# Moving the first attention block's query path into the DFT stage, with the latents' loads and one sequence's output-weight gating

## The chip, the cores and the metric

One core of a Trainium2 chip. The core has a matrix engine (PE, with its weight loads shown as PEld), a vector engine (DVE), an activation engine (ACT), a general engine (POOL) and a sync engine (SP) that here only issues transfers. Each engine takes its instructions in the order of its own queue and waits on semaphores. The metric is the device time of one execution in microseconds.

## The reference

Two sequences of 1024 tokens and width 1024 go through one layer. A conditioning vector gives shift, scale and gate for each half of the layer. Attention (4 heads, low-rank queries and keys, a rotary part) and a 2-D Fourier mixing run side by side on the same normed input:

```
mod = jax.nn.silu(c) @ w_ada + b_ada            # sh1, sc1, ga1, sh2, sc2, ga2
h = rmsnorm(x, g_mix) * (1.0 + sc1) + sh1
z = h @ w_in                                    # q_lat 256, kv_lat 128, k_pe 64, f_in 512
y_mla = mla_group(q_lat, kv_lat, k_pe, ...)     # softmax attention, 4 heads
y_four = fourier_group(f_in, w_four)            # Re(fft2) over tokens and 64 channels, then w_four
x = x + ga1 * (concat(y_mla, y_four) @ w_out)
x = x + ga2 * ((silu(h2 @ w_gate) * (h2 @ w_up)) @ w_down)   # h2: normed and modulated x
```

A last rmsnorm gives the outputs. All is 32-bit floating point.

## The kernel before

Each product is made of three matmuls on values split into a high and a low part: mm3 (lines 70 to 73), and split (59 to 61), in which ACT casts the high part and DVE subtracts to get the low one. The kernel runs in stages that keep their results in DRAM buffers.

Stage 1 (both sequences, 8 pairs of row blocks) norms, transposes and projects. It writes the latents to lat_d (128 partitions, two 128-row pieces of query latents, one of key latents, one of the rotary key), the values to ckv_d, the folded query weights to wq_d, the folded output weights without gate to wo_d, and the gate rows to ga_d.

Stage 2 is the DFT stage (pools p2a on the left of the on-chip memory, p2 and praw on the right). For each sequence s it runs dft(s), prep_wm(s), which loads and splits Fourier output weights through eight "raw" buffers, and fourier_out(s, abn, j) for j = 1, 2, 3, 0 (lines 690 to 719). One fourier_out has two groups g of 13 matmuls into two of eight PSUM banks. ACT copies one bank (ea, L706), DVE forms difference and sum (ed, three buffers each), and SP stores both to fo_d (L719). Beside the first sequence's four steps run the chunks of the second modulation vector (wada2, four buffers of 1 MB in p2a, lines 742 to 749). After dft(1) and prep_wm(1) the left pool is closed, and pool p3e takes its bytes. stage3_loads (lines 581 to 596) then loads the first block's query latents (ql), the query weights wq in two halves through two "hv" buffers with a split each, the rotary tables rc and rs, and, by load_seq(0), the first sequence's latents (2 x 1 MB) and values (2 x 512 KB).

Stage 3 is attention. The items are (sequence, block of 256 rows, head, half): 64 of them. Item k runs scores; one item later its probabilities are transposed (flip_p), then multiplied with the values; out_proj follows 11 items behind. Before the loop, rope_q (L842 to 860) forms the rotary part of the queries of block (0, 0), absorb_q the folded query of head 0, and rope_flip transposes the rotary part. In the loop the same functions run ahead for later blocks. The table todo gives other work to items: at items 0 and 2, gate_half(0, g) loads a gate row of 128 copies into one buffer (gah), and wv_load(0, g) loads four pieces of wo_d and multiplies each with it on POOL (L958, L959); wv_split splits the eight results into wv at items 3 to 10. add_x starts accumulating transfers from POOL.

The order on each queue is not that of the text. A scheduler orders the instructions by priority when the program is built, gives a tile the first buffer of its tag that comes free, and sets the waits. A tile whose buffer is held by another waits for the last user of that one. issue_after(i) places what is under it behind instruction i on its engine. Each transfer also waits until the eighth transfer before it on its queue is done, since eight semaphores go round.

Of the kernel before, what the change touches and what calls it, by code (L numbers as in the profile page):

```python
# [12 lines left out]
F32 = mybir.dt.float32  # L13
# [37 lines left out]
def hybrid_encoder_kernel(ctx: ExitStack, tc: tile.TileContext, a: dict):  # L51
# [513 lines left out]
    def load_seq(s, lp=None):  # L565
        lat = [(e if s == 0 else lp).tile([P, 2, N], F32R, tag=f"lat{s}{i}", name=f"lat{s}{i}") for i in range(2)]
        ckv = [e.tile([P, 8, KVL], F32R, tag=f"ckv{i}", name=f"ckv{i}", bufs=1) for i in range(2)]
        for i in range(2):
            nc.sync.dma_start(rd(lat[i]), lat_d[s][i][:, 2:4, :])
        for i in range(2):  # L570
            nc.sync.dma_start(rd(ckv[i]), ckv_d[s][i])
        S[s] = (lat, ckv)

    def load_q(s, b):
        ql = [e.tile([P, 2, 256], F32R, tag=f"ql{i}", name=f"ql{i}", bufs=2) for i in range(2)]
        for i in range(2):
            nc.sync.dma_start(rd(ql[i]), lat_d[s][i][:, 0:2, 256 * b : 256 * b + 256])
        S["q", s, b] = ql

    def stage3_loads():  # L580
        wq_h = e.tile([P, 2, 768], F32R, name="wq_h")
        wq_l = e.tile([P, 2, 768], F32R, name="wq_l")
        load_q(0, 0)
        for c in range(2):
            wqr = half("wqr")
            wqr2 = half("wqr2")
            nc.sync.dma_start(wqr, wq_d[:, c, 0:512])
            nc.sync.dma_start(wqr2[:, :256], wq_d[:, c, 512:768])
            split(wq_h[:, c, 512:768], wq_l[:, c, 512:768], wqr2[:, :256])
            split(wq_h[:, c, 0:512], wq_l[:, c, 0:512], wqr)  # L590
        rc = e.tile([P, 8, ROPE], F32, name="rc")
        nc.sync.dma_start(rc, a["ropec"])
        rs = e.tile([P, 8, ROPE], F32, name="rs")
        nc.sync.dma_start(rs, a["ropes"])
        load_seq(0)
        return wq_h, wq_l, rc, rs

    with ExitStack() as st:
# [4 lines left out]

        def bank2():
            return pp.tile([P, 512], F32, tag="b", name="bank")

        zh, wms = {}, {}

# [82 lines left out]
        def fourier_out(s, ABn, j):  # L691
# [5 lines left out]
            for g in range(2):  # L697
# [20 lines left out]
                for u in range(2):  # L718
                    nc.sync.dma_start(fo_d[s][rows(j, u), gs], ed[u])  # L719

        zsplit(0)
        tb[1] = [wa.tile([P, 4, 512], F32R, name=f"tb1{i}") for i in range(2)]
        for c in range(4):
# [113 lines left out]
    with ExitStack() as st:  # L837
# [4 lines left out]
        def rope_q(s, b, u):  # L842
            ql = S["q", s, b]
            ti = 2 * b + u
            us = slice(u * P, u * P + P)
            pq = gbank()
            for c in range(2):
                mm3(pq[:, :256], ql[0][:, c, us], ql[1][:, c, us], wq_h[:, c, 512:], wq_l[:, c, 512:], c == 0, c == 1)
            pv = pq[:, :256].rearrange("p (h r) -> p h r", h=HEADS)
            t1 = half("qt1").rearrange("p (k h r) -> p k h r", k=2, h=HEADS)  # L850
            cb = rc[:, ti : ti + 1, :].broadcast_to([P, HEADS, ROPE])
            sb = rs[:, ti : ti + 1, :].broadcast_to([P, HEADS, ROPE])
            nc.vector.tensor_tensor(out=t1[:, 0], in0=pv, in1=cb, op=ALU.mult)
            nc.vector.tensor_tensor(out=t1[:, 1, :, :32], in0=pv[:, :, 32:], in1=sb[:, :, :32], op=ALU.mult)
            nc.vector.tensor_tensor(out=t1[:, 1, :, 32:], in0=pv[:, :, :32], in1=sb[:, :, 32:], op=ALU.mult)
            here["p"] = nc.gpsimd.tensor_tensor(out=t1[:, 0], in0=t1[:, 0], in1=t1[:, 1], op=ALU.add).ins
            sk = w.tile([P, HEADS, P], F32R, tag="sk", name="qsk", bufs=2)
            nc.scalar.copy(sk[:, :, :64], t1[:, 0])
            nc.vector.tensor_tensor(out=sk[:, :, 64:], in0=t1[:, 0], in1=rd(sk[:, :, :64]), op=ALU.subtract)
            S["sk", s, b, u] = sk  # L860

        def rope_flip(s, b, u):
            sk = S.pop(("sk", s, b, u))
            pt = tbank("pqt", F32R)
            for h in range(HEADS):
                nc.tensor.transpose(pt[:, h, :], sk[:, h, :], identr)
            qp = w.tile([P, HEADS, P], F32R, tag="qp", name="qp", bufs=4)
            nc.scalar.copy(qp, rd(pt))
            S["qp", s, b, u] = qp

        def absorb_q(s, b, h):
            ql = S["q", s, b]
            pq = gbank()
            hs = slice(h * P, h * P + P)
            for c in range(2):
                mm3(pq[:, :256], wq_h[:, c, hs], wq_l[:, c, hs], ql[0][:, c, :], ql[1][:, c, :], c == 0, c == 1)
            qa = [w.tile([P, 256], F32R, tag=f"qa{i}", name=f"qa{i}", bufs=3) for i in range(2)]
            split(qa[0], qa[1], pq[:, :256])
            S["qa", s, b, h] = qa

        def scores(s, b, h, u):
            lat = S[s][0]
            qa, qp = S["qa", s, b, h], S["qp", s, b, u]
# [69 lines left out]
        def wv_load(s, g):  # L953
            gs = slice(512 * g, 512 * g + 512)
            raw4 = (w if s == 0 else e).tile([P, 4, 512], F32, tag=f"lat{1 - s}{g}", name="wvr4")
            for h in range(HEADS):
                raw = raw4[:, h, :]
                nc.sync.dma_start(raw, wo_d[:, h, gs])  # L958
                nc.gpsimd.tensor_tensor(out=raw, in0=raw, in1=S["ga"], op=ALU.mult)  # L959
                S["wv", h, g] = raw  # L960

        def wv_split(i):
# [20 lines left out]
        for k in range(nit + 4):  # L983
            if k >= nit:
                i = k - nit
                out_proj(1, 2, i // 2, i % 2)
                if i == 1:
                    norm2(1, 2, 0, tl)
            if k < nit:
                s, b, h, u = items[k]  # L990
                scores(s, b, h, u)
                nxt = items[k + 8 - k % 8] if k + 8 - k % 8 < nit else None
                i = k % 8
                if nxt is not None:
                    if i == 0:
                        load_q(*nxt[:2])
                    if i == 3 and nxt[1] == 0:
                        load_seq(nxt[0], w)
                    if i in (3, 4):
                        rope_q(*nxt[:2], i - 3)  # L1000
                    if i in (5, 6):
                        rope_flip(*nxt[:2], i - 5)
                if u == 1 and k + 1 < nit:
                    absorb_q(*items[k + 1][:3])
# [591 lines left out]
```

## Time and profile before

| what | value |
|---|---|
| runs | 2137.21, 2137.72, 2283.99 us; median 2137.72 |
| profiled execution | 2136.0 us; span from first to last instruction 2134.2 us |
| granted PE clock, mean over the span | 0.989 of full speed |
| DMA rate, mean over the span | 174 GB/s |
| second sequence's Fourier output step on PE | 316.58 to 348.2 us |
| first score matmul of attention | 353.98 us |

A row of the timeline or of a group reads: start and duration in us (or a group's busy time and mean ns), engine, line of the program, operation, output tile, "<-" inputs, shape, count; in square brackets the idle time of that engine just before, and what ended it. In the table of windows the numbers are the stretch, its length, the busy time and count on PE, PEld, DVE, ACT and POOL, the granted PE clock, the DMA share and the GB/s.

### The profile page before, as it was taken

The page shows a single profiled execution, that of the slowest core. Times are in us where ns is not written, and L with a number is a line of the kernel's source. Part 1 is how long each engine was busy: PE and PEld are TensorE (multiplying, and loading weights), DVE is VectorE, ACT ScalarE, POOL GpSimd, SP SyncE. Part 2 cuts the span into 40 slices and gives each one's busy share as a digit, 9 for nine tenths or more (in the row PEclk, how much of TensorE's full clock was granted, in tenths as well). Part 3 has the DMA queues.
Part 4 walks back from the last instruction along what each step waited for, and adds up shares of the span by engine and source line. Part 5 has one row for each costly group of instructions (what it writes and reads, how often), then busy time and mean ns, then how long its engine had stood idle before and what let it go on. Part 6 is the DMA issues. An engine that isn't in the chain of part 4 may idle for free. (4 is left out here: it accounts for less than half of the span.)

```text
span 2134.2 us, 28930 instructions
## 1 busy us (share of the span) xinstructions
PE 2054.9 (96%) x10096; PEld 1671.4 (78%) x10096; DVE 1420.7 (67%) x2118; ACT 904.3 (42%) x1758; POOL 826.7 (39%) x1014
## 2 busy tenths in 40 slices
PE   5899998999999998999999999999999999999998
PEld 3787865888888886888888888887788888888876
DVE  2656655766676668786677667777866566557675
ACT  2655522555564546333333336444333333336441
POOL 1455202111222313797797720135545445420142
PEclk8999999999999999999999999999999999999999
DMA  9586656433545355564455468675423222248662
GB/s 366 189 248 181 225 189 234 102 92 92 138 119 124 119 182 203 187 212 168 159 206 188 153 227 290 226 237 175 148 79 119 99 101 97 99 135 290 230 226 101
DMA packets 184387, 371.11 MB, mean 174 GB/s; under 512 B 19280, under 2 KB 58832, under 8 KB 181168
## 3 DMA queue, kind: packets, MB, share of 16 engines
q1 hardware_dynamic: 166384, 313.80, 44.3%
q0 software_dynamic: 17856, 55.45, 8.8%
q8 instruction: 79, 1.29, 0.2%
q14 instruction: 68, 0.56, 0.1%
HBM read 257.18 MB, written 120.39 MB: 177 GB/s over the span
## 5 line engine op out<-in xcount | busy, mean ns | idle before, releaser
L71 PE MATMUL bank<-H,wh 128*128 128x512 f32 x1232 | 489.4, 397 | 13.5 <-DVE val L130 5.0
L73 PE MATMUL bank<-H,wl 128*128 128x512 f32 x1232 | 488.1, 396 | 1.5 <-DVE wl L61 1.5
L72 PE MATMUL bank<-H,wh 128*128 128x512 f32 x1232 | 488.2, 396 | 0.0
L130 DVE TENSOR_TENSOR val<-bank,val 128x512 f32<-128x512 f32 x244 | 167.0, 689 | 191.2 <-PE bank L73 183.4
L71 PEld LDWEIGHTS bank<-H,wh 128*128 128x128 f32 x1232 | 232.2, 188 | 73.2 <-DVE val L130 7.3
L73 PEld LDWEIGHTS bank<-H,wl 128*128 128x128 f32 x1232 | 232.0, 188 | 58.5 <-DVE wl L61 2.3
L72 PEld LDWEIGHTS bank<-H,wh 128*128 128x128 f32 x1232 | 232.0, 188 | 55.8
L61 DVE TENSOR_TENSOR wl<-draw,wh 128x512 fp32r<-128x512 f32 x286 | 200.9, 737 | 80.9 <-ACT wh L60 79.8
L60 ACT CAST wh<-draw 128x512 fp32r<-128x512 f32 x286 | 169.3, 619 | 155.3 <-PE bank L72 76.9
L72 PE MATMUL bank<-wl,wh 128*128 128x512 f32 x572 | 223.7, 391 | 2.2 <-DVE wl L61 2.2
L130 POOL TENSOR_TENSOR val<-val 128x512 f32<-128x512 f32 x58 | 82.8, 1434 | 363.5 <-DVE val L1380 188.6
L73 PE MATMUL bank<-wh,wl 128*128 128x512 f32 x572 | 222.6, 389 | 0.0
L71 PE MATMUL bank<-wh 128*128 128x512 f32 x572 | 222.6, 389 | 0.0
L60 ACT CAST wh<-rgu 128x512 fp32r<-128x512 f32 x172 | 106.7, 621 | 269.4 <-PE bank L72 211.5
L60 ACT CAST wh<-val 128x512 fp32r<-128x512 f32 x133 | 82.2, 621 | 277.6 <-PE bank L72 249.4
L61 DVE TENSOR_TENSOR wl<-val,wh 128x512 fp32r<-128x512 f32 x133 | 139.3, 1049 | 83.5 <-ACT wh L60 83.5
L61 DVE TENSOR_TENSOR wl<-rgu,wh 128x512 fp32r<-128x512 f32 x172 | 167.1, 972 | 4.8 <-ACT wh L60 4.2
L127 POOL TENSOR_TENSOR val<-rgu 128x512 f32<-128x512 f32 x84 | 122.0, 1452 | 120.3 <-DMA rgu<-in_wgu_dram 92.5
L72 PEld LDWEIGHTS bank<-wl,wh 128*128 128x128 f32 x572 | 107.3, 188 | 27.7 <-DVE wl L61 5.7
L71 PEld LDWEIGHTS bank<-wh 128*128 128x128 f32 x572 | 107.4, 188 | 22.3
L73 PEld LDWEIGHTS bank<-wh,wl 128*128 128x128 f32 x572 | 107.4, 188 | 22.1
L127 POOL TENSOR_TENSOR val<-val 128x512 f32<-128x512 f32 x89 | 119.4, 1358 | 1.3
(319 smaller groups left out, 4096.7 us busy)
## 6 DMA issues: line engine op xcount, KB each, us to landing
rgu<-in_wgu_dram SPq DMA_DIRECT2D x86, 512.0 KB, 4.2
draw<-s_d SPq DMA_DIRECT2D x143, 256.0 KB, 4.1
s_d<-val POOLq DMA_DIRECT2D x88, 256.0 KB, 4.1
draw<-t_d SPq DMA_DIRECT2D x88, 256.0 KB, 4.3
s_d<-val SPq DMA_DIRECT2D x66, 256.0 KB, 2.7
draw<-in_w_down_dram SPq DMA_DIRECT2D x55, 256.0 KB, 4.0
wada<-in_w_ada_dram SPq DMA_DIRECT2D x13, 1024.0 KB, 8.8
xt<-in_x_dram SPq DMA_DIRECT2D x16, 512.0 KB, 6.3
```

The costliest lines, as they stand in the source:

```text
L60: here["a"] = nc.scalar.copy(hi, src).ins
L61: here["v"] = nc.vector.tensor_tensor(out=lo, in0=src, in1=rd(hi), op=ALU.subtract).ins
L71: nc.tensor.matmul(out, lh, rh, start=first, stop=False, skip_group_check=cont)
L72: nc.tensor.matmul(out, lh, rl, start=False, stop=False, skip_group_check=cont)
L73: nc.tensor.matmul(out, ll, rh, start=False, stop=last, skip_group_check=cont)
L127: eng.tensor_tensor(out=out, in0=x, in1=y, op=ALU.subtract)
L130: eng.tensor_tensor(out=out, in0=x, in1=y, op=ALU.add)
```

## The change

It has three parts.

1. rope_q, absorb_q and rope_flip are lifted out of stage 3 and take the PSUM bank function as an argument. Block (0, 0)'s calls now stand in the second sequence's loop of fourier_out: rope_q for both halves after j = 2, absorb_q and rope_flip after j = 3. Their tiles (sk, qp, qa) move from pool p3 to p3e.
2. stage3_loads first reserves the places of the small tiles, so that the latents fall on the bytes of the wada2 chunks, then calls load_seq(0), then the new gate_wo, and only then loads ql, wq, rc and rs.
3. gate_wo loads both gate rows of the first sequence and the eight pieces of wo_d through the raw buffers, multiplies on POOL behind a tiny placing addition that reads the last part of dft(1)'s result, and stores them from POOL to a new DRAM buffer wog_d. wv_load(0, g) reads wog_d and no longer multiplies; both halves are asked for at item 0, and gate_half(0, g) is gone. (The words of the change call it sequence 1; it is index 0.)

```
+    wog_d = dram.tile([P, 4, D], F32, name="wog_d")
...
-    def stage3_loads():
+    def stage3_loads(gate_wo, gate_after):
         wq_h = e.tile([P, 2, 768], F32R, name="wq_h")
         wq_l = e.tile([P, 2, 768], F32R, name="wq_l")
+        for tag, n, bufs in (("ql0", 512, 2), ("ql1", 512, 2), ("hv", 512, 2), ("rc", 512, 1), ("rs", 512, 1), ("sk", 512, 2),
+                             ("gah", 512, 1), ("qa0", 256, 3), ("qa1", 256, 3)):
+            e.tile([P, n], F32, tag=tag, name=tag, bufs=bufs)
+        load_seq(0)
+        gate_wo(gate_after)
         load_q(0, 0)
...
-        load_seq(0)
         return wq_h, wq_l, rc, rs
...
+        def gate_wo(after):
+
+            pc = tiny.tile([P, 1], F32, name="pc")
+            place = nc.gpsimd.tensor_tensor(out=pc, in0=after, in1=after, op=ALU.add).ins
+            ga = [raw_tile("gar")[:, :512] for _ in range(2)]
+            for g in range(2):
+                nc.sync.dma_start(ga[g], ga_d[32 * g, :].partition_broadcast(P))
+            for g in range(2):
+                gs = slice(512 * g, 512 * g + 512)
+                for h in range(HEADS):
+                    r = raw_tile("wor")[:, :512]
+                    nc.sync.dma_start(r, wo_d[:, h, gs])
+                    with tc.issue_after(place):
+                        nc.gpsimd.tensor_tensor(out=r, in0=r, in1=ga[g], op=ALU.mult)
+                        nc.gpsimd.dma_start(wog_d[:, h, gs], r)
...
         for s in range(2):
             for j in (1, 2, 3, 0):
                 fourier_out(s, abn, j)
+                if s == 1 and j == 2:
+                    for u in range(2):
+                        rope_q(0, 0, u, bank2)
+                if s == 1 and j == 3:
+                    absorb_q(0, 0, 0, bank2)
+                    for u in range(2):
+                        rope_flip(0, 0, u, bank2t)
...
-                wq_h, wq_l, rc, rs = stage3_loads()
+                wq_h, wq_l, rc, rs = stage3_loads(gate_wo, rd(abn[1][1][:, 1, 0:1]))
...
-        for u in range(2):
-            rope_q(0, 0, u)
-        absorb_q(0, 0, 0)
-        for u in range(2):
-            rope_flip(0, 0, u)
...
-                nc.sync.dma_start(raw, wo_d[:, h, gs])
-                nc.gpsimd.tensor_tensor(out=raw, in0=raw, in1=S["ga"], op=ALU.mult)
+                nc.sync.dma_start(raw, (wog_d if s == 0 else wo_d)[:, h, gs])
+                if s == 1:
+                    nc.gpsimd.tensor_tensor(out=raw, in0=raw, in1=S["ga"], op=ALU.mult)
...
-            todo[2 * g].append(lambda g=g: gate_half(0, g))
-            todo[2 * g].append(lambda g=g: wv_load(0, g))
+            todo[0].append(lambda g=g: wv_load(0, g))
```

In the built program the affected stretch of SP's queue has this order. Before: ..., two fo_d stores, two ql, wqr and wqr2 (first half of wq), rc, rs, the first latents, wqr and wqr2 (second half), the second latents, two ckv, twelve fo_d stores, ... After: ..., two gate rows, one fo_d store, six wor, one fo_d store, the seventh wor, both latents, two ckv, the eighth wor, two ql, wqr and wqr2, rc, rs, two fo_d stores, wqr and wqr2, five fo_d stores, two ql, eight fo_d stores, eight gated pieces. On PE the first rope_q matmul stands after the fourth of the second sequence's eight groups, and the 12 matmuls of rope_q are mixed into the fifth.

More of the change, by code (lines that the diff above doesn't have):

```diff
@@ L578, in load_q, with rope_q @@
         S["q", s, b] = ql
-    def stage3_loads():
+    def rope_q(s, b, u, bankf):
+        ql = S["q", s, b]
+        ti = 2 * b + u
+        us = slice(u * P, u * P + P)
+        pq = bankf()
+        for c in range(2):
+            mm3(pq[:, :256], ql[0][:, c, us], ql[1][:, c, us], wq_h[:, c, 512:], wq_l[:, c, 512:], c == 0, c == 1)
+        pv = pq[:, :256].rearrange("p (h r) -> p h r", h=HEADS)
+        t1 = half("qt1").rearrange("p (k h r) -> p k h r", k=2, h=HEADS)
+        cb = rc[:, ti : ti + 1, :].broadcast_to([P, HEADS, ROPE])
+        sb = rs[:, ti : ti + 1, :].broadcast_to([P, HEADS, ROPE])
+        nc.vector.tensor_tensor(out=t1[:, 0], in0=pv, in1=cb, op=ALU.mult)
+        nc.vector.tensor_tensor(out=t1[:, 1, :, :32], in0=pv[:, :, 32:], in1=sb[:, :, :32], op=ALU.mult)
+        nc.vector.tensor_tensor(out=t1[:, 1, :, 32:], in0=pv[:, :, :32], in1=sb[:, :, 32:], op=ALU.mult)
+        here["p"] = nc.gpsimd.tensor_tensor(out=t1[:, 0], in0=t1[:, 0], in1=t1[:, 1], op=ALU.add).ins
+        sk = e.tile([P, HEADS, P], F32R, tag="sk", name="qsk", bufs=2)
+        nc.scalar.copy(sk[:, :, :64], t1[:, 0])
+        nc.vector.tensor_tensor(out=sk[:, :, 64:], in0=t1[:, 0], in1=rd(sk[:, :, :64]), op=ALU.subtract)
+        S["sk", s, b, u] = sk
@@ new lines, in rope_flip, with absorb_q @@
+    def rope_flip(s, b, u, bankf):
+        sk = S.pop(("sk", s, b, u))
+        pt = bankf("pqt", F32R)
+        for h in range(HEADS):
+            nc.tensor.transpose(pt[:, h, :], sk[:, h, :], identr)
+        qp = e.tile([P, HEADS, P], F32R, tag="qp", name="qp", bufs=4)
+        nc.scalar.copy(qp, rd(pt))
+        S["qp", s, b, u] = qp
+    def absorb_q(s, b, h, bankf):
+        ql = S["q", s, b]
+        pq = bankf()
+        hs = slice(h * P, h * P + P)
+        for c in range(2):
+            mm3(pq[:, :256], wq_h[:, c, hs], wq_l[:, c, hs], ql[0][:, c, :], ql[1][:, c, :], c == 0, c == 1)
+        qa = [e.tile([P, 256], F32R, tag=f"qa{i}", name=f"qa{i}", bufs=3) for i in range(2)]
+        split(qa[0], qa[1], pq[:, :256])
+        S["qa", s, b, h] = qa
@@ L840, in hybrid_encoder_kernel @@
         st.enter_context(E3)
[L842 to L879, printed above, removed]
         def scores(s, b, h, u):
```

13 lines of the change are left out of this document (8 added, 5 removed).

## The prediction

> **What bounds the kernel now.** I read the page first, then the matmul engine's own rows around the change. The work is PE's: it is busy for 96% of the span, so only idle or slowed PE time can be won.
>
> ```profile
> span 2134.2 us, 28930 instructions
> ## 1 busy us (share of the span) xinstructions
> PE 2054.9 (96%) x10096; PEld 1671.4 (78%) x10096; DVE 1420.7 (67%) x2118; ACT 904.3 (42%) x1758; POOL 826.7 (39%) x1014
> ```
>
> The table of windows (columns: stretch, length, busy time by engine, granted clock, DMA share, GB/s) holds the stretches I need.
>
> ```profile
> 312.00:321.00 9.00, 9.00 (x40) 6.88 (x39) 6.13 (x26) 2.38 (x4) 0.00 (x0) 1.00 0.03 6
> 326.00:341.00 15.00, 15.00 (x59) 10.22 (x58) 4.54 (x8) 4.21 (x9) 0.00 (x0) 1.00 0.98 348
> 348.20:380.00 31.80, 22.45 (x103) 17.67 (x104) 21.38 (x41) 14.49 (x27) 14.39 (x11) 0.84 0.49 162
> 365.10:371.70 6.60, 5.55 (x19) 4.27 (x18) 4.11 (x6) 1.40 (x4) 6.32 (x5) 0.50 0.03 10
> 375.40:378.60 3.20, 3.20 (x11) 2.68 (x11) 3.20 (x6) 2.57 (x5) 0.00 (x0) 0.50 0.62 252
> ```
>
> The DFT stage (312 to 341) keeps PE full at clock 1.00. Attention's start (348.2 to 380) does not: PE is idle for 31.80 - 22.45 = 9.35 us, and in two stretches its clock is 0.50. PE's timeline names the pieces of it.
>
> ```profile
> 349.47 0.39 PE L71 MATMUL gb<-wq_h,ql 128*128 128x256 f32 x1 [1.29 <-DVE ed L130]
> ...
> 364.59 0.36 PE L71 MATMUL gb<-ql,wq_h 128*128 128x256 f32 x1 [2.77 <-DVE qt L855]
> ...
> 374.84 1.71 PE L915 MATMUL ppt<-ident,p 128*128 128x128 f32 x8 [2.03 <-DVE pt L61]
> ```
>
> The last of them comes from POOL: its eight gating multiplies stand before a rotary addition (qt, L856), and ACT waits 5.88 us in its queue for that.
>
> ```profile
> 351.92 0.73 POOL L856 TENSOR_TENSOR qt<-qt 128x256 f32<-128x256 f32 x1 [110.42 <-DVE qt L855]
> 354.08 0.74 POOL L856 TENSOR_TENSOR qt<-qt 128x256 f32<-128x256 f32 x1 [1.43 <-DVE qt L855]
> 356.02 5.96 POOL L959 TENSOR_TENSOR wvr<-wvr,gah 128x512 f32<-128x512 f32 x4 [1.20 <-DMA wvr<-wo_d]
> 365.38 6.27 POOL L959 TENSOR_TENSOR wvr<-wvr,gah 128x512 f32<-128x512 f32 x4 [3.41 <-DMA gah<-ga_d]
> 371.61 0.73 POOL L856 TENSOR_TENSOR qt<-qt 128x256 f32<-128x256 f32 x1
> ```
> ```profile
> 372.38 0.41 ACT L858 CAST qsk<-qt 128x256 fp32r<-128x256 f32 x1 [5.88 <-POOL qt L856]
> ```
>
> **What the change can win.** The first block's query work, 12 matmuls for rope_q, 6 for absorb_q and 8 flips, is not removed. It moves into PE's stream in the DFT stage, at the same price. What can go is its waiting: the 9.35 us and the slow clock. Part of the idle time stays, because the first flip of probabilities needs a whole softmax.
>
> ```profile
> 362.64 1.28 ACT L901 ACT_TABLE_LOAD   x1
> 363.94 1.11 ACT L901 ACTIVATE p<-ps_s,nb 128x1024 f32<-128x1024 f32 x1
> 364.95 0.19 ACT L901 ACTIVATION_READ_ACCUMULATOR p<-ps_s,nb 128x1 f32 x1
> ```
> ```profile
> L898 DVE TENSOR_REDUCE mx<-ps_s 128x1 f32<-128x1024 f32 x22 | 26.9, 1221 | 15.5 <-PE ps_s L893 15.5
> L903 DVE TENSOR_SCALAR p<-p,rr 128x1024 f32<-128x1024 f32 x22 | 18.4, 835 | 0.5
> ```
>
> That chain is 1.22 + 1.28 + 1.11 + 0.19 + 0.84 = 4.64 us. PE can meanwhile do the next item's scores (10 matmuls, 0.233 us start to start, 2.3 us) and 12 half-width matmuls of the next queries (0.117 us each, 1.4 us). That leaves 0.9 us, with handovers about 1.5. So 9.35 - 1.5 = **7.9 us of idle time goes** (bounds 5 and 9.35). At clock 0.50 half of PE's busy time is lost: 5.55 / 2 = 2.8 in the first stretch, which follows the 2.77 us wait and goes with it, and 3.20 / 2 = 1.6 in the second, which I let stay for the gap that stays. So **2.8 us of clock goes** (bounds 0 and 4.4). Gain together: 10.7 us.
>
> The twelve microseconds of POOL multiplies are no longer attention's. In the DFT stage POOL has nothing else to do (0.00 busy in the windows above), and nobody there waits for it, with one exception that is next. If that cover were gone, the 12.2 us would stand in front of qt as they do now.
>
> **What the change can lose.** Here the order of the built program matters, which the diff does not tell. On SP's queue the seventh load of raw output weights ("wor") stands before the latents, both ckv halves, the eighth wor, the two ql and the four wq loads. The raw pool has eight buffers and ten tiles are asked for, so the seventh wor takes the first gate row's buffer. The built program lets it wait on POOL, for the fourth multiply, and the multiplies begin when B's low part of the second sequence's DFT is written.
>
> ```profile
> 317.05 0.69 DVE L61 TENSOR_TENSOR B<-bank,B 128x512 fp32r<-128x512 f32 x1
> ```
> ```profile
> 398.13 1.05 POOL L560 DMA_DIRECT2D fo_d<-in_x_dram  x1
> ```
>
> POOL: 317.74, then the tiny placing add (0.2), four multiplies (5.96) and between them two store issues (1.05 each): 326.0. Before the change SP went straight on:
>
> ```profile
> 321.07 0.99 SPq L719 DMA_DIRECT2D fo_d<-ed  x2
> 322.24 0.92 SPq L577 DMA_DIRECT2D ql<-lat_d  x2
> 323.21 0.46 SPq L587 DMA_DIRECT2D wqr<-wq_d  x1
> 323.72 0.43 SPq L588 DMA_DIRECT2D wqr<-wq_d  x1
> 324.19 0.43 SPq L592 DMA_DIRECT2D rc<-in_ropec_dram  x1
> 324.67 0.42 SPq L594 DMA_DIRECT2D rs<-in_ropes_dram  x1
> 325.14 0.43 SPq L569 DMA_DIRECT2D lat<-lat_d  x1
> 329.09 0.33 SPq L587 DMA_DIRECT2D wqr<-wq_d  x1
> ```
>
> Its first wqr was issued at 323.21, ahead of both latents and both ckv. Now it is issued at 326.0 plus nine issues, and its data come behind 256 (wor) + 2 x 1024 (latents) + 2 x 512 (ckv) + 256 (wor) + 2 x 256 (ql) KB. With its own 256 and 128 KB that is 4480 KB, 4.59 MB. Four of POOL's gated stores, 256 KB each, are issued in the same time: 5.64 MB. The queue's rate when it is full is the 348 GB/s of 326 to 341, so the bytes take 16.2 us. A single transfer's overhead is what its shortest landing leaves beside its bytes:
>
> ```profile
> DMA to landing us min/median/max: 2.0/2.9/9.4
> ```
>
> 2.0 less 0.75 for 256 KB, 1.25 us. So the first half of wq lands at 326.0 + 1.25 + 16.2 = 343.4. PE needs its casts too:
>
> ```profile
> L60 ACT CAST wq_h<-wqr x4: 401/514/622, 327.3 to 333.4; 128x512 fp32r<-128x512 f32 x2, 128x256 fp32r<-128x256 f32 x2
> L61 DVE TENSOR_TENSOR wq_l<-wqr,wq_h x4: 419/554/693, 328.4 to 334.1; 128x512 fp32r<-128x512 f32 x2, 128x256 fp32r<-128x256 f32 x2
> ```
>
> 0.62 + 0.40 makes 344.5. PE's stream has the first rope_q matmul after the fourth of eight groups of the second sequence's output step, where the fifth starts now:
>
> ```profile
> 330.33 0.39 PE L71 MATMUL bank<-wm,A 128*128 128x512 f32 x1
> ```
>
> PE takes matmuls in order, so everything behind stands: **first wait 344.5 - 330.33 = 14.2 us.** The second half of wq reuses the staging buffers of the first and is issued 329.09 - 323.21 = 5.9 us after it. Between the two PE has 6 half-width and 10 full matmuls, 3.0 us: **second wait 2.9 us** (bounds 0 and 5.9; at half clock the 3.0 us become up to 6 and fill the same time). Loss: 17.1 us.
>
> Other moved work. The gate rows and the first six wor loads are issued as raw buffers come free, before 312, and land in a queue that is nearly empty (6 GB/s from 312 to 321): nothing to pay. The output stores (fo_d) behind the late loads hold ed buffers, three deep; PE is standing anyway. The eight gated reloads come after the last fo_d, when the weights are needed three items later; I cost them at nothing, and one late reload would cost about one 2 us gap. POOL's ports: a multiply beside DVE work takes 6.27 / 4 instead of 5.96 / 4, 0.1 us each, nothing.
>
> The Trainium skill, page "TensorE: Matmul & The Clock Gate", Part 1, says that the clock halves after an idle window of about 3.4 us and is restored by one busy window of that length. The trace is harsher: a wait of 2.77 us was enough, and 0.50 was held for 6.6 us although PE was busy for 5.55 of them. By the page the restart after the 14.2 us would cost at most 1.7 us, by the row 2.8; either hides in the wait for the second half, so the sum is the same within 1 us.
>
> **Sum.** +14.2 + 2.9 - 7.9 - 2.8 = +6.4 us. The profiled execution took 2136.0 us (span 2134.2), so 2142.4; the median shown, 2137.72, lies 1.7 above it, so **2144 us** as a median. Fast end: full gains (13.75) and 4.59 MB at 423 GB/s with no stores in the way, first wait 8.8: -2.0, 2136. Slow end: second wait 5.9, only 5 us of idle and no clock won: +15.1, 2153.
>
> **Rivals.** (1) The loads keep ahead of PE, and the change does what its words say: -10.7, 2127. For it: the queue is empty from 312 to 321 and the latents' new bytes are free long before. Against it: SP's order. It decides when both waits fall under 10.7 us, that is when the first half is usable at 338.1 instead of 344.5.
>
> (2) The queue runs at its best, not its mean. One view of the DMA work has single slices at 423:
>
> ```profile
> GB/s 392 423 387 83 312 206 325 221 317 370 290 251 285 255 296 99 87 5 0 16 3 0 221 321 381 317 304 347 399 341 188 287 286 309 237 4 173 0 0 139
> ```
>
> 5.64 MB then take 13.3 us, first wait 11.3, +3.5, 2141. The full stretch's 348 over 15 us speaks against it. The Trainium skill, page "DMA: Bandwidth & Descriptors", under "Where 436 GB/s comes from", gives 435 GB/s as the fabric's ceiling; by that estimate it would be 2141 too.
>
> (3) Attention's idle time comes from the softmax chain alone and stays, slow clock included: +17.1, 2155. For it: the chain is 4.64 us. Against it: qt (POOL, DVE) ends the two longest waits or stands before them.
>
> **Chances.** Forecast 0.63 (2136 to 2153), rival 2 0.15 (inside that range), rival 1 0.10, rival 3 0.10, something over 2% 0.02. Range 2135 to 2153, which leaves out rival 1, most of rival 3 and the rest. Two per cent, 43 us, is about what a measurement of this kernel can tell from no change; every case above is inside it: faster 0.01, same 0.96, slower 0.03.
>
> **What would show it.** In the profile after: an idle gap of 9 to 18 us on PE before the first matmul of wq_h and ql, near 330 to 345, ended by ACT's cast of wq_h, and a short one for the second half; SP's latent loads issued at about 326; clock 0.50 behind the gap; the 2.77 and 2.03 us gaps gone and 1 to 2 us before the first flip left. I am wrong if wq lands before 338, if PE's gap is not there, or if attention starts with as much idle time as now.

## The result and the profile after

The kernel after takes 2142.78 us (median of 22 runs, 2139.79 to 2147.9), the kernel before on the same chips 2138.98 us (22 runs, 2136.71 up; one disturbed run of 2283.99 is left out of the ratio). The ratio is 1.002 with a 95% interval of 1.0015 to 1.0026: slower by 3.8 us by the medians (3.2 to 5.6 us by the interval), well inside 2%. Forecast were 2144 us and a loss of 6.4 us. The loss is the safer comparison, since the runs of before lie 1.3 us higher here than in the three that the forecast started from. The profiled executions differ by the same 3.8 us: 2139.79 after, 2136.0 before.

The head of the page after, and the table of windows after (same columns as above):

```profile
span 2138.0 us, 28976 instructions
```
```profile
312.00:321.00 9.00, 9.00 (x41) 6.90 (x40) 6.91 (x22) 2.38 (x4) 2.57 (x3) 1.00 0.06 19
325.88:342.99 17.11, 5.22 (x20) 3.40 (x19) 6.19 (x7) 1.18 (x2) 7.85 (x10) 0.71 0.97 358
331.20:343.90 12.70, 0.00 (x0) 0.00 (x0) 1.13 (x3) 0.91 (x2) 2.63 (x4) 0.58 1.03 398
343.90:346.50 2.60, 2.53 (x9) 2.40 (x10) 1.46 (x3) 0.01 (x1) 0.00 (x0) 0.50 0.97 331
360.00:380.00 20.00, 18.27 (x90) 13.27 (x90) 15.37 (x29) 10.01 (x19) 0.73 (x1) 1.00 0.46 158
```

PE does nothing from 331.2 to 343.9, while the DMA engines run full at 398 GB/s: the transform stage, which had no idle time there before, now waits for data. In exchange the start of the attention is nearly clean, at clock 1.00. PE's timeline names each wait; these four are all that is left between 326 and 400:

```profile
343.97 0.80 PE L71 MATMUL bank<-wq_h,ql 128*128 128x256 f32 x2 [12.87 <-ACT wq_h L60]
...
366.47 0.50 PE L920 MATMUL ps_s<-lat,qa 128*128 128x512 f32 x1 [0.29 <-DVE ed L131]
...
374.17 1.09 PE L946 MATMUL ppt<-ident,p 128*128 128x128 f32 x8 [1.44 <-DVE p L934]
...
383.43 1.06 PE L946 MATMUL ppt<-ident,p 128*128 128x128 f32 x8 [0.43 <-DVE nb L930]
```

The first is the forecast wait: the first query matmul, released by ACT's cast of wq_h, which itself waited for the transfer. SP's queue shows why the transfer was late:

```profile
322.72 0.32 SPq L766 DMA_DIRECT2D fo_d<-ed  x1
325.47 0.32 SPq L779 DMA_DIRECT2D wor<-wo_d  x1
325.88 0.89 SPq L570 DMA_DIRECT2D lat<-lat_d  x2
...
329.90 0.58 SPq L632 DMA_DIRECT2D wqr<-wq_d  x1
...
344.36 0.32 SPq L632 DMA_DIRECT2D wqr<-wq_d  x1
```
```profile
342.99 0.92 ACT L60 CAST wq_h<-wqr 128x512 fp32r<-128x512 f32 x2 [12.82 <-DMA wqr<-wq_d]
...
347.77 0.93 ACT L60 CAST wq_h<-wqr 128x512 fp32r<-128x512 f32 x2 [3.86 <-DMA wqr<-wq_d]
```

The seventh load of output weights goes at 325.47, the latents right behind it, the query weights at 329.90 with 3 MB of latents and values ahead of them, and they are cast 13 us later. What the forecast had not seen is on DVE, beside POOL's multiplies:

```profile
322.01 0.67 DVE L128 TENSOR_TENSOR ed<-ea,bank 128x512 f32<-128x512 f32 x1
322.61 2.87 DVE L148 TENSOR_SCALAR s<-s 128x8 f32<-128x8 f32 x1
325.39 0.68 DVE L131 TENSOR_TENSOR ed<-ea,bank 128x512 f32<-128x512 f32 x1
325.99 3.09 DVE L149 TENSOR_TENSOR s<-s,gT 128x8 f32<-128x8 f32 x1
```
```profile
322.88 2.56 POOL L781 TENSOR_TENSOR wor<-wor,gar 128x512 f32<-128x512 f32 x2
...
326.51 2.54 POOL L781 TENSOR_TENSOR wor<-wor,gar 128x512 f32<-128x512 f32 x2
```

Two operations on 8 elements a partition take 2.87 and 3.09 us. They end at 325.48 and 329.08, POOL's pairs of multiplies at 325.44 and 329.05, and the rows of the transform (ed) stand behind them in DVE's queue. In this kernel SP has only the first row to store before the latents, and that was formed ahead of both operations. So here it is the seventh load that holds SP, until the fourth multiply ends at 325.44.

### The profile page after: what moved, and what is told of

Its sections match the earlier page's. It is cut to its first block, busy times and chain, and to the rows that moved or that the text cites. A ratio compares the mean times of both kernels' runs of the same rounds, so it can differ in the third digit from the quotient of the medians.

```text
span 2138.0 us, 28976 instructions
## 1 busy us (share of the span) xinstructions
PE 2052.2 (96%) x10096; PEld 1671.0 (78%) x10096; DVE 1424.4 (67%) x2118; ACT 902.5 (42%) x1758; POOL 831.2 (39%) x1023
## 3 DMA queue, kind: packets, MB, share of 16 engines
q8 instruction: 79, 1.29, 0.2%
```

## The experiments

The theory behind the forecast, called A, and D once the blocked DVE had been added: PE stands where it meets a query matmul, because SP's queue holds the query weights behind POOL's multiplies (through the seventh load, and in D also through DVE's rows, where SP has to store more than one of them first) and behind 3 MB of latents and values. The rivals: B, the same bytes have to pass in any order; C, POOL's multiplies and the queue of the row stores are the loss, not the order of the loads; E, the gain is the gating's, not the query path's. G, F, H and J are local to single runs. "Rows" are ed, the second sequence's transform results, stored to fo_d. The sequence whose output weights are gated early is the one with index 0, the change's "sequence 1". Ratios are to the kernel before, with 95% intervals.

### Order of the loads and POOL's wait, apart and together

**wq_first** puts query latents and weights ahead again; the new lines keep the latents' places:

```
-        load_seq(0)
-        gate_wo(gate_after)
+        for i in range(2):
+            e.tile([P, 2, N], F32R, tag=f"lat0{i}", name=f"lat0{i}")
+        for i in range(2):
+            e.tile([P, 8, KVL], F32R, tag=f"ckv{i}", name=f"ckv{i}", bufs=1)
         load_q(0, 0)
...
+        load_seq(0)
+        gate_wo(gate_after)
         return wq_h, wq_l, rc, rs
```

> Only the order of SP's loads is changed: query latents, query weights and the rope tables go ahead of the latents and values of sequence 0 again, as in the kernel before; gating, bytes and the place of the query matmuls stay as in the kernel after. SP still stands for POOL at its seventh load of output weights (325.5 us in the profile after). Theory A (what PE waited for is the 3 MB ahead of the query weights): behind that load go only 0.5 MB of query latents and 0.4 MB of weights, 2.3 us at the 394 GB/s of the profile after, and a landing of some 4 us as in the profile before; the weights are there at 330 to 332, split a microsecond later, and PE's 12.87 us wait shrinks to 1 to 4 us: 8 to 10 us faster than the kernel after, so some 2134 us, 4 to 6 us faster than the kernel before. Rival B (the same bytes have to pass in any order, and the wait only moves to the first scores, which then wait for the latents): the first score starts no earlier than the 366.5 us of the profile after, and the time stays at 2141 to 2144. Rival C (the loss is POOL's multiplies on SP's queue: the eighth load now stands ahead of the stores of the transform's rows, and these hold PE through the three buffers of ed and the eight banks): PE still stands 5 us or more in 330 to 350, and the time is no better than the kernel before, 2138 to 2141.

Measured: 2142.02 us, ratio 1.0021 (1.0011 to 1.003). The wait shrank as A said, the time did not.

```profile
337.87 0.39 PE L71 MATMUL bank<-wq_h,ql 128*128 128x256 f32 x1 [3.79 <-ACT wq_h L60]
...
365.70 0.50 PE L924 MATMUL ps_s<-lat,qa 128*128 128x512 f32 x1 [2.85 <-DVE ed L128]
...
376.09 1.21 PE L950 MATMUL ppt<-ident,p 128*128 128x128 f32 x8 [2.52 <-DVE p L938]
```
```profile
340.78 0.50 SPq L783 DMA_DIRECT2D wor<-wo_d  x1
341.32 20.74 SPq L770 DMA_DIRECT2D fo_d<-ed  x13
```

The first score waits 2.85 us for DVE's last rows, not for the latents, so B's mechanism is not there although its time is. Fifteen of the sixteen row stores still stand on SP behind these loads, thirteen of them in one stretch from 341.32 on. The last rows leave DVE late, and the first softmax comes late too (2.52 us where the kernel after waits 1.44). Even so PE's waits from 330 to 390 come to 11.2 us in this execution, against 15.0 in the kernel after. The clock takes the difference:

```profile
339.20:342.60 3.40, 3.40 (x10) 1.98 (x8) 0.00 (x0) 0.00 (x0) 0.00 (x0) 0.53 1.04 417
366.70:370.10 3.40, 3.40 (x9) 2.64 (x8) 0.54 (x1) 0.00 (x0) 0.00 (x0) 0.50 0.85 256
376.60:380.20 3.60, 3.60 (x14) 2.92 (x13) 3.21 (x6) 3.60 (x8) 0.51 (x1) 0.55 0.02 5
```

At about half clock, these 10.4 us of PE lose 4.9, against 1.3 in the kernel after. Removing the largest wait by itself let the next ones show, and each of three waits cost a stretch of slow clock.

**gate6** gates six tiles early and two in the attention, so that no load waits for a multiply (the second gate row is loaded there too):

```
-                for h in range(HEADS):
+                for h in range(HEADS - 2 * g):
                     r = raw_tile("wor")[:, :512]
...
-                if s == 1:
+                if s == 1 or h >= HEADS - 2 * g:
                     nc.gpsimd.tensor_tensor(out=raw, in0=raw, in1=S["ga"], op=ALU.mult)
```

> Six of the eight tiles of output weights are gated in the transform stage instead of eight; the last two are gated in the attention by POOL, as the kernel before does with all eight. The two gates and six tiles fill the eight raw buffers, so no load on SP waits for a multiply of POOL, and 0.5 MB of loads and 0.5 MB of stores less pass in this stretch. The latents stay ahead of the query weights. Theory A: the latents are issued behind the first store of ed at 322.7 instead of 325.9 (3.1 us), and 0.5 MB less stands ahead (1.3 us at 394 GB/s), so the query weights land 4 to 5.5 us earlier, and PE's first wait shrinks from 12.87 to 7.5 to 9 us: some 2138 us, the time of the kernel before within 2 us. Rival C (POOL's wait on SP's queue is the whole loss): the wait goes almost entirely, and the time is 2130 to 2133. Rival B (bytes bind): 1.3 to 2.6 us less, 2140 to 2142.

Measured: 2145.03 us, 1.0044 (1.003 to 1.0058): slower than the kernel after, and no theory expected that. PE's wait is 11.84 us. SP was freed of POOL's fourth multiply and then stood for the second row, which DVE formed only after its blocked operation:

```profile
322.29 3.69 SPq L766 DMA_DIRECT2D fo_d<-ed  x2
326.08 0.91 SPq L570 DMA_DIRECT2D lat<-lat_d  x2
```
```profile
322.18 2.87 DVE L148 TENSOR_SCALAR s<-s 128x8 f32<-128x8 f32 x1
324.96 0.68 DVE L131 TENSOR_TENSOR ed<-ea,bank 128x512 f32<-128x512 f32 x1
```
```profile
342.50:351.30 8.80, 8.79 (x25) 0.50 0.86 298
```

The latents went at 326.08 instead of 325.88: one wait on POOL had been exchanged for another. The last row (PE alone) is PE after its wait: at clock 0.50 for 8.8 us where the kernel after has it for 2.6 us. Half of the busy time is 4.4 us against 1.3, so 3.1 us more. By the ratios the two kernels lie 5 us apart, and PE's wait is 1 us shorter here: some 3 us are open. They arise late: the flips of the eighth item start 2.1 us later than in the kernel after (409.88 and 407.81), the last matmul 5 us later (2132.60 and 2127.55), and far behind the edit I have no row for them.

**gate6_wq** joins both edits.

> Both edits together: query latents and weights ahead of the latents of sequence 0, and six tiles gated in the transform stage, so that no load on SP waits for POOL. Theory A: SP's queue is that of the kernel before up to the query weights, whose halves were split there at 327.3 to 328.9 and at 333.4 to 334.5; the first query matmul after the fourth group (330.7 to 331) finds the first half, its second half waits at most some 3 us. The 9.35 us of idle time at the start of the attention go except for 2 us, and the slow clock with them: the first score starts at 354 to 357 less 8, some 8 us faster than the kernel before, 2131 us (2128 to 2134). Rival B (bytes): the latents come after the scores want them, and a wait of 4 us or more stands ahead of the first score: 2135 to 2139. Rival C: the idle time at the start of the attention comes back behind other names (split probabilities, banks), as in the third rival of the prediction: 2136 or more.

Measured: 2133.04 us, 0.9982 (0.9973 to 0.999), faster than the kernel before. Against gate6 only the order of the loads differs, and it gives 12 us and takes PE's wait from 11.84 to 2.19 us. The time is A's:

```profile
334.63 0.38 PE L71 MATMUL bank<-wq_h,ql 128*128 128x256 f32 x1 [2.19 <-ACT wq_h L60]
...
341.17 0.51 PE L71 MATMUL bank<-wq_h,ql 128*128 128x256 f32 x2 [0.43 <-ACT wq_h L60]
```

A had expected no wait for the first half. SP issues the query latents only at 327.86 here, behind the second row's store, which stands for DVE as in gate6.

**q_back** leaves gating and latents as in the kernel after, and moves the calls of rope_q, absorb_q and rope_flip back ahead of the attention's items.

> The query path of the first block is back at the start of the attention; gating in the transform stage and the latents ahead of the query weights stay as in the kernel after. Theory A (PE stands only where it meets a query matmul): the transform runs through without a wait as in the kernel before, the query weights (split at 343 and 349 in the profile after) hold the attention's first matmul for 1 to 2 us, and its other waits come back, less what POOL no longer does there: 2138 to 2141, the time of the kernel before within 2 us. Rival C (SP's queue holds PE without any query matmul): the stores of the transform's rows stand behind the same loads until 340 to 345 in the profile after, three buffers of ed and eight banks are full by the sixth or seventh group, and PE stands some 5 us in 337 to 348 for a bank that DVE hasn't emptied: 2142 to 2146, no faster than the kernel after.

Measured: 2138.39 us, 1.0004 (0.9996 to 1.0013). The time is A's, but C's mechanism is there in part: PE stands 3.79 us in the transform without a query matmul in its stream, for a bank that DVE could not empty. DVE stood in its queue for two things one after the other: for the split of the query weights, which had not come, and then 0.72 us for a row buffer whose store was late.

```profile
347.75 0.50 PE L71 MATMUL bank<-wm,A 128*128 128x512 f32 x1 [3.79 <-DVE ed L131]
```
```profile
345.25 1.03 DVE L61 TENSOR_TENSOR wq_l<-wqr,wq_h 128x512 fp32r<-128x512 f32 x2 [12.48 <-ACT wq_h L60]
347.01 0.69 DVE L131 TENSOR_TENSOR ed<-ea,bank 128x512 f32<-128x512 f32 x1 [0.72 <-DMA fo_d<-ed]
```

### What POOL's multiplies cost, and what each part gives

**no_mult** is the kernel after without line 781: the gate of that sequence's attention output is left out, the loads and stores remain.

```
-                        nc.gpsimd.tensor_tensor(out=r, in0=r, in1=ga[g], op=ALU.mult)
                         nc.gpsimd.dma_start(wog_d[:, h, gs], r)
```

> The kernel after without the eight multiplies on POOL: the output weights of sequence 1 are loaded and stored again as they are, so the gate of sequence 1's attention output is left out. All loads, stores and their places in the queues stay, and no load on SP waits for a multiply. The first runs showed two operations on vectors of 128x8 at 2.87 and 3.09 us on DVE beside POOL's multiplies (0.17 us in the profile before), ahead of the first rows of the transform that SP stores. Theory D (POOL's multiplies block DVE, and through it and through the seventh load they hold SP's queue; behind that come the 3 MB of latents and values): the two operations take 0.2 us again, both first stores are issued by 322, the latents 3 to 4 us earlier than the 325.9 of the profile after, PE's wait for the query weights shrinks from 12.87 to 9 or 10 us, and the time is 2138 to 2140.5. Rival G (the long operations of DVE have another cause, such as the issue of the stores on POOL): they stay at 2.9 us, the second store still goes at 325 or later, and the time is within 1 us of the kernel after.

Measured: 2137.79 us, 1.0003 (0.9994 to 1.0012), 3.6 us faster than the kernel after by the ratios. PE's wait is 8.87 us. On DVE (this whole execution stands 5.6 us later from before the stage on; the low part of B starts at 323.21, 317.66 in the kernel after):

```profile
327.13 0.16 DVE L148 TENSOR_SCALAR s<-s 128x8 f32<-128x8 f32 x1
327.20 0.68 DVE L131 TENSOR_TENSOR ed<-ea,bank 128x512 f32<-128x512 f32 x1
327.80 0.16 DVE L149 TENSOR_TENSOR s<-s,gT 128x8 f32<-128x8 f32 x1
```

POOL's stores are all there and DVE is not blocked; so it was the multiplies (D), not the issue of the stores (G). Nearly the whole loss of the change went with them. This run takes away both of their effects, the wait of the seventh load and the held DVE, and does not tell them apart.

**no_gate** undoes the gating alone. In stage3_loads the call of gate_wo is gone, wv_load multiplies on POOL as before, and latents stay ahead of the query weights.

> The gating is back in the attention as in the kernel before; the query path stays in the transform stage and the latents stay ahead of the query weights. No multiply, load or store of output weights is left in the transform stage. Theory D: the latents go behind the first two stores at 322; 3.5 MB stand ahead of the first half of the query weights, 9 us at 394 GB/s, and with landing and split they are usable at 335 to 337: PE waits 4 to 7 us for them, and the latents' order alone costs that. The gates come back as work in the attention: 2139 to 2143, slower than the kernel before by 1 to 5 us. Rival E (POOL's multiplies on the queue are the whole loss, the order of the latents costs nothing): no wait over 1.5 us in the transform stage, 2130 to 2134.

Measured: 2145.25 us, 1.0036 (1.0024 to 1.0047). The wait is D's, the time is worse than D's:

```profile
338.23 0.79 PE L71 MATMUL bank<-wq_h,ql 128*128 128x256 f32 x2 [6.19 <-ACT wq_h L60]
...
383.59 0.58 PE L919 MATMUL ps_s<-lat,qa 128*128 128x512 f32 x1 [3.81 <-ACT qa L60]
```

The order of the latents costs 6.19 us without any POOL work near; the second row is a wait at the start of the attention that the multiplies bring back. What the forecast of this run left out is the clock: in this execution it is 0.50 to 0.51 behind the waits of 6.19, 2.50 and 3.81 us, for 4.5, 3.4 and 7.0 us.

**nogate_wq4** is the query path's move by itself, with its loads first and four staging buffers:

```
-            wqr = half("wqr")
-            wqr2 = half("wqr2")
+            wqr, wqr2 = [half(n) if c == 0 else e.tile([P, 512], F32, tag="sk", name=n, bufs=2) for n in ("wqr", "wqr2")]
```

> The query path's move by itself: gating back in the attention, query latents and weights ahead of the latents as in the kernel before, and the second half of the query weights in two buffers of its own (those of qsk), so that it needn't wait for the split of the first. Theory D: SP's queue is that of the kernel before, both halves are split by 331, the query matmuls after the fourth group find them, and no wait over 1 us is left in the transform stage; the waits of 2.77 and 2.03 us and the slow clock at the start of the attention go in part, while the waits for the gates' multiplies stay: 2131 to 2136, 2 to 6 us faster than the kernel before. Rival E (what the change gains comes from the gating, and the query path's move only shifts the idle time to the first scores): 2137 to 2140.

Measured: 2136.03 us, 0.9992 (0.9983 to 1.0001), at D's slow edge. No wait is left in the transform, but one of 6.78 us stands in the attention:

```profile
375.46 0.79 PE L922 MATMUL ps_s<-lat,qa 128*128 128x512 f32 x1 [6.78 <-ACT qa L60]
```
```profile
366.70 0.41 ACT L597 CAST qsk<-qt 128x256 fp32r<-128x256 f32 x1 [3.32 <-POOL qt L595]
...
370.85 0.62 ACT L60 CAST wv<-wvr 128x512 fp32r<-128x512 f32 x1 [2.17 <-POOL wvr L987]
...
375.04 0.36 ACT L60 CAST qa<-gb 128x256 fp32r<-128x256 f32 x1
```

ACT stands for POOL twice, for a rotary addition behind the first four multiplies and with a cast of wv for the next four, and the cast of qa, for which PE waits, is behind both. That is what the gating's move takes away. PE's waits at the attention's start come to 9.65 us here (9.37 in the kernel before): the query path alone only shifts them, as E had it.

**gate_dve_wq4** has all three parts, with the multiplies on DVE (line 781 with nc.vector), the query loads first and the four buffers.

> All three parts of the change with three edits: the eight multiplies are DVE's instead of POOL's, query latents and weights go ahead of the latents, and the second half of the query weights has two buffers of its own. Theory D: nothing of POOL is left in SP's queue and nothing blocks DVE; both halves of the query weights are split by 332, PE waits under 1 us for them; the idle time at the start of the attention is down to some 2 us as in the profile after: 2127 to 2131, 7 to 11 us faster than the kernel before. Rival F (eight more multiplies of 128x512 on DVE, 0.67 us each by the rows of the same shape, 5.4 us, stand ahead of the transform's splits and rows): PE waits for DVE for 2 us or more in 316 to 360, 2131 to 2135.

Measured: 2134.14 us, 0.9983 (0.9975 to 0.9992). No wait in the transform exceeds 0.47 us, so D is right there, but the time is F's, and so is a wait of 2.08 us at the stage's end:

```profile
355.88 0.50 PE L923 MATMUL ps_s<-lat,qa 128*128 128x512 f32 x1 [2.08 <-DVE ed L131]
```

F's reason is not shown: the last of the eight multiplies on DVE is over at 327.6. DVE stands later, 4.26 us for ACT's cast of qa and then 0.54 us for a row's store (row at 343.64), and thirteen of the row stores are still on SP behind the loads.

### The queue of the row stores

**gate6_wq4** is gate6_wq with the four staging buffers.

> As the run gate6_wq (six tiles gated by POOL in the transform stage, query latents and weights ahead of the latents), with two buffers of its own for the second half of the query weights. Theory D: all four parts of the query weights are issued together at some 328 and land together; the second half no longer waits for the split of the first (6 us apart in gate6_wq), but the first lands up to 1 us later for it. PE's waits in the transform stage come to 2 to 3 us in one piece, against 2.19 + 0.29 + 0.43 + 0.49 in gate6_wq: within 1.5 us of it, 2131.5 to 2134. Rival J (the second half was what set the flips and the end of the stage): 3 us or more faster than gate6_wq.

Measured: 2133.24 us, 0.9985 (0.9977 to 0.9994), like gate6_wq; J falls. Its profiled execution was the slowest of its runs, 2141.54 us, which the last section uses.

**gate6_wq4_act** issues the second sequence's row stores from ACT:

```
-                    nc.sync.dma_start(fo_d[s][rows(j, u), gs], ed[u])
+                    (nc.scalar if s == 1 else nc.sync).dma_start(fo_d[s][rows(j, u), gs], ed[u])
```

> As gate6_wq4, with the stores of the rows of sequence 1's transform issued from ACT's queue instead of SP's. Theory D (SP's loads stood behind the first two of these stores, which waited for DVE, which POOL's multiplies blocked): the query loads are issued when their bytes come free, at 316 to 320, in the stretch that moved only 19 GB/s in the profile after; both halves are split before the fourth group ends, PE waits for nothing over 0.5 us in the transform stage, and its idle time at the start of the attention stays at 2 us or less: 2127 to 2131, 2 to 5 us faster than gate6_wq4. Rival H (a store on ACT waits for DVE's row, and what stands behind it on ACT waits too: copies out of the banks and splits of the query weights): waits of 2 us or more for ACT, 2133 or more.

Measured: 2131.04 us, 0.9975 (0.9965 to 0.9984), the slow edge of D's range. SP issues the query latents at 317.93 instead of 328.74 (gate6_wq4), yet waits of 1.04, 0.45 and 0.76 us remain, ended by ACT and DVE, which POOL still blocks: some of H.

**gate6_dve_wq4_act** takes the six multiplies to DVE as well.

> As gate6_wq4_act, with the six multiplies on DVE instead of POOL. Theory D: DVE's two blocked operations (2.9 and 3.1 us) go, its rows of the transform come 5 us earlier, six multiplies of 0.67 us take the place of idle time ahead of 320: 0 to 2 us faster than gate6_wq4_act, 2126 to 2131. Rival F (the DVE stands later than PE at the end of the transform, as in the run gate_dve_wq4, where the first scores waited 2.08 us for its last rows): no faster than gate6_wq4_act, 2131 to 2134.

Measured: 2128.67 us, 0.9959 (0.9947 to 0.9971), the fastest of all, 2.4 us under the run before it (five runs; the two intervals just overlap). F falls.

```profile
318.09 0.88 SPq L578 DMA_DIRECT2D ql<-lat_d  x2
```
```profile
321.00:345.00 24.00, 24.00 (x108) 17.54 (x108) 14.08 (x44) 7.13 (x15) 4.00 (x7) 1.00 0.98 365
345.00:352.70 7.70, 7.70 (x31) 3.38 (x29) 4.93 (x8) 0.58 (x1) 0.00 (x0) 1.00 0.61 229
```

PE is busy for 24.00 of 24.00 and 7.70 of 7.70 us at clock 1.00, up to the first score at 352.73 (366.47 in the kernel after, 353.98 before), and the query work is done.

**before_act** is the control, the kernel before with only that edit of the stores.

> A control: the kernel before with only the stores of sequence 1's rows issued from ACT's queue. If the gains of the two runs above are the change's with its queue set right, this edit by itself gives nothing, since no instruction of the kernel before waits for a load of this stretch before the attention begins: 2136 to 2140, within 2 us of the kernel before. If the queue of the stores is a cost of its own, whatever stands behind it, it is faster by 2 us or more: under 2136.

Measured: 2133.65 us, 0.998 (0.9971 to 0.9989). My control was expected to show nothing and gained 4 us. The queue of the stores is a cost of its own, and the kernel before already paid it. In the kernel before DVE stands 6.63 us ahead of the rows of its fifth group for a buffer whose store was behind the latents; in the control these rows wait for no store:

```profile
341.19 0.69 DVE L127 TENSOR_TENSOR ed<-ea,bank 128x512 f32<-128x512 f32 x1 [6.63 <-DMA fo_d<-ed]
```
```profile
335.87 0.69 DVE L127 TENSOR_TENSOR ed<-ea,bank 128x512 f32<-128x512 f32 x1 [2.13 <-issue]
```

The last rows then leave DVE in time: the 1.29 us for which PE waited for them at 349.47 are gone, and PE's waits at the attention's start come to 6.6 us instead of 9.4. So of the 9.0 us that the best kernel gains, some 4 can be had without the change, and some 5 (2133.65 less 2128.67) are the change's with its loads in the right order and its multiplies off POOL, six of eight tiles gated early. The shares hold for this order of adding them: on top of gate6_wq4 the stores' queue gave 2.2 us, not 4.

## Why the prediction was right, step by step

- **First wait, 14.2 us forecast, 12.87 measured.** The place (behind the fourth group, whose last matmul starts at 330.71), the cause and the releaser were right. That the order of the loads costs this is shown by gate6 against gate6_wq (11.84 to 2.19 us) and by wq_first (12.87 to 3.79); no_gate against nogate_wq4 (6.19 us against none) agrees, but there the four staging buffers differ too. SP was clear at 325.47 (326.0 forecast), since POOL's store issues took 0.56 to 0.6 us each, not the 1.05 of another transfer's row. The first half of the weights was there at 342.99 (343.4 forecast): the mean rate from the first latents' issue to then was 358 GB/s, near the 348 assumed, and 398 only in the gap itself. Of the 1.3 us that the wait is shorter, 0.8 are PE's, which came to it at 331.10 instead of 330.33, and 0.5 the weights'.
- **Second wait, 2.9 us forecast, none measured.** The lower bound came true: PE had 343.97 to 348.81 to fill, it filled it with interleaved group work, and 2.53 us of that ran at half clock (1.3 us lost).
- **Idle time at the attention's start, 7.9 us gained by forecast.** 9.35 us were there, 0.29 + 1.44 + 0.43 = 2.16 are left: 7.2 gained. The chain of the first softmax (1.44) is what stayed, as forecast (1.5).
- **Slow clock, 2.8 us gained by forecast.** Both stretches at 0.50 went, also the second, which I had let stay: 4.4 us.
- **The sum.** 12.87 + 1.3 - 7.2 - 4.4 = +2.6, forecast +6.4. Measured were +3.8; 0.6 of it stands already ahead of this stage (the low part of B at 317.66, before 317.05). The rows do not add up to the rest: the flips of the eighth item start 2.35 us later than before (407.81 and 405.46), where the sum and the 0.6 make 3.2, and 1.4 us more arise behind them, for which I have no row.
- **POOL's ports, "0.1 us each, nothing": this step failed, though it cost the kernel after little that a row shows.** I took the price from long multiplies in the attention and looked at what POOL's operations cost, not at whom they stop. In the kernel after they stop DVE for 2.9 and 3.1 us. There the wait of SP's seventh load, which I had counted, hid it: the one row stored ahead of the latents was formed before. gate6 took that wait away, SP then stood for the blocked second row, and PE gained 1 us of its 12.87. With the multiplies gone (no_mult), and with them both waits, PE's wait falls by 4.0 us and the time by 3.6. No run takes the blocked DVE away by itself.
- **"The output stores behind the late loads hold ed buffers; PE is standing anyway": half right.** It is so in the kernel after. But without the query matmuls (q_back) PE stands 3.79 us in the transform, in part for those buffers, and in the kernel before the stores' queue cost 4 us that I had not seen, though the 6.63 us were in its trace.
- **Rivals.** Rival 1 (the loads keep ahead, 2127) is nearly reached once the queues are set right, 2133.04 with two edits and 2128.67 with five, but some 4 us of that can be had without the change. Rival 2 is out, though its +3.5 is nearest to the measured loss: the mean of 358 GB/s is close to my 348, not to its 423. Rival 3 is out: 2.16 us of idle time are left, at full clock.

## What to carry to other kernels

Read a change to loads on every queue that it touches: an engine that issues transfers in order stands for its slowest waiter, and here a store that waited for DVE, DVE that waited for POOL, and a load that waited for POOL stood one behind the other, so that removing one of them gained next to nothing against the kernel after (wq_first) or lost (gate6), and removing all made a kernel 9 us faster than the one before. Look for stores of late results on the queue that loads the next stage: moving them gave 4 and 2.2 us here. A multiply that POOL does "for nothing" beside DVE should be priced by what DVE has in its queue at that moment.

## What the runs showed of the hardware that I had not expected

**POOL's multiplies hold some of DVE's operations, and not others.** Beside them a 128x8 operation on on-chip memory took 2.87 or 3.09 us (0.16 without them), and it ended with the pair of multiplies, not with the first of it. The rows ed, one of whose inputs is a PSUM bank, kept their 0.67 us, also the two (330.20 and 330.80) that ran inside a multiply (330.12 to 331.42). The Trainium skill, page "SBUF — State Buffer", section "SBUF: two separate sides", states such a rule: GpSimd and DVE hold a shared pair of ports exclusively for a whole instruction, and DVE needs it for two inputs from SBUF or in a two-port mode. The traces agree in what is held and what is not. They do not show who came first: by the records both held operations begin before the pairs, by 0.27 and 0.52 us.

**Nearly the same wait costs the clock nothing or several microseconds.** gate6_wq and gate6_wq4 wait nearly alike before their query matmuls (2.19 + 0.29 and 2.10 + 0.37 us). In gate6_wq4 the clock then falls, at 336.6, and a third wait of 0.80 us follows; in gate6_wq it does not fall. First gate6_wq, then gate6_wq4 (rows of PE alone):

```profile
334.60:338.00 3.40, 3.08 (x14) 1.00 1.06 433
```
```profile
337.50:346.70 9.20, 9.20 (x25) 0.50 1.02 417
```

Runs of gate6_wq4 spread from 2130.75 to 2141.54 us around 2133.24. In gate6 the clock stayed at 0.50 for 8.8 us with PE busy for 8.79 of them. The Trainium skill, page "TensorE: Matmul & The Clock Gate", Part 1, has one busy window of some 3.4 us restore the clock, with free-running windows. By that, where a window begins could explain the difference between the first two kernels, which no run here shows; it does not explain the 8.8 and 9.2 us, where the measurement decides. One profile is therefore not a measure of a wait's cost here; the medians are.
